# Hybrid encoder trunk on one core: passes of seven products that go on from chunk to chunk, and two pairs of the last chunk that join them

## The chip, the core and the metric

One core of one Trainium2 chip runs the whole program. The metric is the time of one execution on the device in microseconds (us), the median of three runs. Besides, one execution was recorded by the hardware profiler; its rows are what is called the trace here.

## What is computed

The reference is a trunk of two encoder layers on an input of 256 positions by 2048 channels, all in float32. Layer 0 mixes by multi-scale pooling and grouped-query attention, layer 1 by a bidirectional mLSTM. The mixers are not touched by the change. Each layer ends in a gated feed-forward block of width D_FF = 5632:

```python
def conv_ffn(x, w_up, conv_w, conv_b, w_down):
    u = x @ w_up
    up = jnp.pad(u, ((0, 0), (1, 1), (0, 0)))
    c = conv_w.astype(u.dtype)
    u = c[0] * up[:, :-2] + c[1] * up[:, 1:-1] + c[2] * up[:, 2:] + conv_b.astype(u.dtype)
    gate, val = jnp.split(u, 2, axis=-1)
    return (jax.nn.silu(gate) * val) @ w_down
```

`x = x + conv_ffn(rms_norm(x, norm_ffn[layer]), ...)` stands at the end of each layer. The change concerns the last product, the one with `w_down`, of 256 x 5632 by 5632 x 2048.

## The kernel before

**Numbers.** A float32 operand is held as two fp32r parts, a high part and a low rest. A product of two such operands is three matmuls: high by high, high by low, low by high.

**Weights.** All weights come in pieces of 128 x 1024 through one stream (class `Stream`, lines 86 to 151). `load` (line 95) issues a DMA on SP into one of six buffers, five pieces ahead of the piece in use. `split` (line 116) makes the two parts: a cast on ScalarE (line 127) and a subtraction on VectorE (line 128) into one of four `hl` buffers, two pieces ahead. The order of the pieces is fixed when the program is written, by `_ffn_weights` (line 1286).

**The feed-forward block.** `ffn_layer` (line 960) follows a plan that `_ffn_plan` (line 1232) writes out. The 5632 inner channels are 44 tiles in six chunks (`FCH`, line 33: 4, 8, 8, 8, 8, 8). An entry "up" makes one tile: 64 matmuls (`stat_group`), then on VectorE and ScalarE the sum of the parts (L427, L428), the norm's factor (L984), the convolution (L989 to L993), the gate (L997, L998) and the two parts of the result (L999, L1000). Every chunk's products with `w_down` are done one chunk later, between the up-tiles of the next chunk, so that weights and vector work are spread.

**Seven products for eight.** For a chunk in `BOTH` (line 35) both halves of the 2048 output columns, for the other chunks only half 1, are computed in the Strassen-Winograd manner: two tiles (a pair) by two blocks of 512 columns by two blocks of 128 positions, with seven products in place of eight. The entry "mix" (`combine`, line 1002) makes the sums of activations of one pair: four subtractions and additions on VectorE (L1006 to L1008) and their parts (L1012 on ScalarE, L1013 on VectorE). The sums of weights are made in two ways. For half 1 a DMA on SP loads one block and an accumulating DMA on POOL adds the other (class `Sum`, `prepare`, line 110, three buffers, up to ten pieces ahead); then VectorE adds that sum to the next piece twice (class `Chain`, L123 and L124). For half 0 they are premixed: `premix` (line 464) lets DMAs on the ScalarE queue and on POOL write them to memory ahead of time, paced by TensorE's progress, and the stream loads them like other weights.

**Passes A and B.** `unit` (line 1023) does the products of one or two pairs. A pass of kind A needs products 4, 6, 5, 3 and holds four PSUM banks, one of kind B needs 0, 1, 2 and holds three. The pool `ps` has four banks (line 226), so one pass is open at a time. A pass begins with the first pair of a chunk and ends with its last; then `drain` (line 1056) empties its banks on VectorE, one operation of 128 x 512 each (L1068; the first pass of a kind and half is copied on ScalarE instead, L1066, except where x takes it), into four running sums `acc` and into x. The next pass waits until the banks are free. For a chunk with both halves the order is A1 A1 B1 B1 A0 A0 B0 B0 (the digit is the half; each unit has two pairs and follows one up-tile; the up-tile with its unit is called a slot and has the up-tile's number). For a chunk with half 1 alone each unit has one pair, A four times and B four times, and after the second and fourth A unit one block of half 0 is done directly (`down`, line 1117).

**The end of the block.** The last chunk's four output blocks of 512 columns are done directly. `down_two` (line 1133) does blocks 0 and 1, first six tiles of each, then the last two, and `down` the blocks 2 and 3, 48 matmuls each; in layer 1 block 3 is done by `down_end` (line 1089), which stores each half as soon as it is ready. `total` (line 1078), eight additions on VectorE, brings the running sums of a half into x, after its last B pass; a block is added to x only behind the total of its half. In layer 0 each finished block of x is squared (L337), transposed on TensorE (L315) and split (L327, L330) for the next layer (`Norm`, line 304).

**Order.** TensorE's order is the program's. Drains, totals and norm steps are small tasks that a weave (line 154) puts between matmuls by a clock of its own. VectorE's, ScalarE's, SP's and POOL's orders are set by the framework's scheduler when the program is built; each engine then works in order.

Of the kernel before, what the change touches and what calls it, by code (L numbers as in the profile page):

```python
# [9 lines left out]
F32 = mybir.dt.float32  # L10
# [22 lines left out]
FCH = [4, 8, 8, 8, 8, 8]  # L33
CH = 8
BOTH = ((0, 2, 3, 4), (0, 1, 2, 3, 4))
NEG = -1.0e30
NGATE = 96 + 8
WARM = 5
# [47 lines left out]
class Stream:  # L86
# [123 lines left out]
def trunk(ctx: ExitStack, tc: tile.TileContext, gx, xT, xn, call, catt, cml, weights, mixes, out):  # L210
# [749 lines left out]
    def ffn_layer(layer, norm, nxt):  # L960
        with ExitStack() as es:
# [4 lines left out]
            st.sums = lp(f"ffs{layer}", 2)  # L966

            acc = kp.tile([P, 2, 4, 512], F32, tag="acc", name=f"acc{layer}")
            combos, pss, quads, seen = {}, {}, {}, set()

            conv = kp.tile([P, NC_CONV], F32, tag="conv", name=f"conv{layer}")
            a.dma_start(conv, call[:, NC_ALL + layer * NC_CONV : NC_ALL + (layer + 1) * NC_CONV])
# [47 lines left out]
                mm(ps, xl, wh, False, last)  # L1020
                wv.tick(0.68)

            def unit(kind, c, h, js):

                n = FCH[c] // 2
                order = (4, 6, 5, 3) if kind == "A" else (0, 1, 2)
                if js[0] == 0:
                    wv.until(lambda: "busy" not in pss)
                    for e in order:
                        pss[e] = psp.tile([P, 512], F32, tag="ps", name=f"pp{layer}_{c}_{h}{e}")  # L1030
                gt = gts[c]

                def part(j, k, t):
                    return [gt[:, 2 * j + k, i, t * P : t * P + P] for i in range(2)]


                todo = []
                for j in js:
                    s3, s1 = combos[c, j]
                    if kind == "A":  # L1040
                        xs = [[s3[:, i, m] for i in range(2)] for m in (1, 0, 2)] + [part(j, 1, 1)]
                    else:
                        xs = [part(j, 0, 0), part(j, 1, 0)]
                    todo += [(e, x_, j) for e, x_ in zip(order, xs)]
                if kind == "B":
                    todo += [(2, [combos[c, j][1][:, i] for i in range(2)], j) for j in js]
                for m, (e, x_, j) in enumerate(todo):
                    if m % 2 == 0:
                        hl = st.next()
                    wh, wl = (hl[:, i, m % 2 * 512 : m % 2 * 512 + 512] for i in range(2))  # L1050
                    product(pss[e], x_, wh, wl, j == 0, j == n - 1)
                if js[-1] == n - 1:
                    pss["busy"] = True
                    wv.add(drain(kind, c, h, order), 0.6)

            def drain(kind, c, h, order):

                x00, x01, x10, _ = parts_of_x(h)
                if kind == "A":
                    steps = [(acc[:, h, k], v.tensor_add, e) for k, e in enumerate(order[:3])]  # L1060
                    steps.append((x10, v.tensor_add, 3))
                else:
                    steps = [(acc[:, h, 3], v.tensor_add, 0), (x00, v.tensor_add, 1), (x01, v.tensor_sub, 2)]
                for to, op, e in steps:
                    if e in (4, 6, 5, 0) and (kind, h) not in seen:
                        a.copy(to, pss[e])  # L1066
                    else:
                        tc.keep_in_program_order(op(to, to, pss[e]))  # L1068
                    yield 1.6
                del pss["busy"]  # L1070
                seen.add((kind, h))
                if kind == "B" and c == len(FCH) - 2:
                    wv.add(total(h), 1.5)

            def parts_of_x(h):
# [40 lines left out]

            def down(c, b):
                gt, last = gts[c], c == len(FCH) - 1
                kts = list(range(FCH[c]))
                if last and nxt is None and b == NB - 1:  # L1120
                    down_end(gt, b, kts)
                    return
                ps = mmp.tile([P, 2, 512], F32, tag="mm", name=f"dn{layer}_{c}_{b}")
                mov_part(ps, lambda k: gt[:, k], kts, True, True)
                if last:
                    wv.until(lambda: ("total", 1) in pss)
                residual(ps, b)
                if last and nxt is None:
                    nc.sync.dma_start(out[:, :, b * 512 : b * 512 + 512], x[:, :, b * 512 : b * 512 + 512])
                elif last:  # L1130
                    nxt.add(b)

            def down_two(c):

                gt, n = gts[c], FCH[c]
                pss2 = [mmp.tile([P, 2, 512], F32, tag="mm", name=f"dn{layer}_{c}_{b}") for b in range(2)]
                for kts in (range(n - 2), range(n - 2, n)):
                    for ps in pss2:
                        mov_part(ps, lambda k: gt[:, k], list(kts), kts[0] == 0, kts[-1] == n - 1)
                wv.until(lambda: ("A", 0) not in seen or ("total", 0) in pss)  # L1140
                for b, ps in enumerate(pss2):
                    residual(ps, b)
                    if nxt is None:
                        nc.sync.dma_start(out[:, :, b * 512 : b * 512 + 512], x[:, :, b * 512 : b * 512 + 512])
                    else:
                        nxt.add(b)
# [3 lines left out]
            for kind, c, i, *j in _ffn_plan(layer):  # L1150
                if kind == "up":
                    if i == 0:
                        gts.append(actp.tile([P, 8, 2, S], F32R, tag=f"B{c % 2}", name=f"g{layer}_{c}"))
                    up(c, f, gts[c], i)
                    f += 1
                    if layer == 0 and c == len(FCH) - 1 and i == 4:
                        premix(1, 30.0, 30.0, 0)
                elif kind == "down":
                    down(c, i)
                elif kind == "two":  # L1160
                    down_two(c)
                elif kind == "mix":
                    combine(c, i)
                else:
                    unit(kind, c, i, *j)
# [19 lines left out]
def _mov(w):  # L1185

    return w.reshape(-1, 2, P, 512).transpose(0, 2, 1, 3).reshape(-1, P, CH * P)
# [38 lines left out]

def _halves(layer, c):

    return () if c in (-1, len(FCH) - 1) else (0, 1) if c in BOTH[layer] else (1,)


def _ffn_plan(layer):

    seq = []
    for c, n in enumerate(FCH):
        pairs = FCH[c - 1] // 2 if c else 0  # L1240
        halves = _halves(layer, c - 1)

        if halves == (0, 1):
            slots = [[(kind, c - 1, h, js)] for h in (1, 0) for kind in "AB"
                     for js in ((0, 1), (2, 3))[: pairs // 2]]
            slots = [[]] * (pairs < 4) + slots
        else:
            slots = [[(kind, c - 1, 1, (j,))] for kind in "AB" for j in range(pairs)]
            for b in range(2 if pairs else 0):
                slots[(b + 1) * pairs // 2 - 1].append(("down", c - 1, b))  # L1250

        busy = {j: k for k, slot in enumerate(slots) for u in slot if u[0] == "A" for j in u[3]}
        for i in range(n):
            seq.append(("up", c, i))
            seq += slots[i] if i < len(slots) else []
            if c < len(FCH) - 1:
                seq += [("mix", c, j) for j in range(n // 2) if i == max(2 * j + 1, busy.get(j, 0))]
    return seq + [("two", len(FCH) - 1, 0)] + [("down", len(FCH) - 1, b) for b in range(2, NB)]


def _down_chunks(layer, w):


    out, k0 = [], 0
    for c, n in enumerate(FCH):
        rows = w[k0 * P : (k0 + n) * P]
        blocks = [_mov(rows[:, b * 512 : b * 512 + 512]) for b in range(NB) if b // 2 not in _halves(layer, c)]
        if c == len(FCH) - 1:
            b0, b1 = blocks[:2]
            blocks[:2] = [b0[:-1], b1[:-1], b0[-1:], b1[-1:]]  # L1270
        out += blocks
        k0 += n
    n = sum(FCH[:-1]) // 2
# [12 lines left out]
def _ffn_weights(layer, up, parts):  # L1286
# [3 lines left out]
    for kind, c, i, *j in _ffn_plan(layer):  # L1290
# [1 line left out]
            out += up[u : u + 4]  # L1292
            u += 4
        elif kind in ("down", "two"):
            out += [next(down) for _ in range(FCH[c] // 2 * (2 if kind == "two" else 1))]
# [119 lines left out]
```

## Time and profile before

| | us |
|---|---|
| median of three runs | 2163.43 |
| lowest and highest | 2162.89, 2163.73 |
| the profiled execution | 2163.78 |
| span of its trace | 2162.0 |
| feed-forward block of layer 0 in the trace, about | 257 to 972 |
| feed-forward block of layer 1 in the trace, about | 1450 to 2162 |

In the profile PE is TensorE's matmuls, PEld its weight loads, DVE VectorE, ACT ScalarE, POOL GpSimd, SP the queue that issues most loads. L128 is line 128 of the kernel before. Tiles bear the program's names without numbers: `up` an up-tile's banks, `pp` those of a pass, `dn` and `end` those of direct blocks, `hl` a split piece of weights, `xt` a transposed piece of x, `xx` its parts. A row of the chain of waits says start, length and what worked; touching pieces of PE mean that TensorE waited for nothing.

### The profile page before, as it was taken

The numbers are of one execution on the slowest core, as the hardware profiler recorded it, in microseconds if no ns is written. First come the engines' busy times: TensorE is split into PE (matmuls) and PEld (weight loads), VectorE is DVE, ScalarE is ACT, GpSimd is POOL, SyncE is SP. The second block draws the span as 40 slices with busy tenths as digits, with TensorE's granted clock in tenths as the row PEclk, the third lists the DMA queues.
The fourth block names the chain that finished last, engine by engine and source line by source line (L and its number), as shares of the span: only waits on it lengthen the run. The fifth ranks groups of instructions, "written<-read, shape, count | busy, mean of one in ns | idle before, by whom it ended". The sixth has DMA issues, their size and how long they took to land.

```text
span 2162.0 us, 31902 instructions
## 1 busy us (share of the span) xinstructions
PE 2156.2 (100%) x11412; PEld 1844.2 (85%) x11412; DVE 1734.7 (80%) x2425; ACT 1414.3 (65%) x2208; POOL 212.7 (10%) x268
## 2 busy tenths in 40 slices
PE   9999999999999999999999999999999999999999
PEld 7888888888888888889888888888888888888887
DVE  7686688887988988986777676667889898988896
ACT  7665578766777767666454544457777777776763
POOL 0022111110100100001111111211100000000000
PEclk9999999999999999999999999999999999999999
DMA  9668989898999877779888888898978787887774
GB/s 323 213 202 250 287 250 311 248 280 247 298 296 293 287 257 232 266 232 252 231 246 251 237 250 230 273 276 249 289 226 285 258 283 246 265 262 251 233 249 162
DMA packets 164097, 555.29 MB, mean 257 GB/s; under 512 B 20602, under 2 KB 23202, under 8 KB 163938
## 3 DMA queue, kind: packets, MB, share of 16 engines
q1 hardware_dynamic: 129632, 462.88, 62.0%
q0 software_dynamic: 20704, 52.71, 14.8%
q10 hardware_dynamic: 13602, 37.67, 5.7%
q8 instruction: 89, 1.46, 0.3%
q14 instruction: 70, 0.57, 0.1%
HBM read 551.04 MB, written 69.25 MB: 287 GB/s over the span
## 4 chain that ended last, share of the span: by engine, by line
PE 97%; DVE 2%; DMA 1%; issue 0%; ACT 0%; DVEq 0%
PE up L264 44%; PE pp L264 15%; PE op L264 8%; PE dn L264 5%; PE mv L264 4%; PE mq L264 4%; PE mk L264 4%; PE mo L264 4%; PE qproj L264 3%; PE kproj L264 1%; PE vproj L264 1%; PE pool L264 1%; DVE hl L128 1%; PE qk L264 1%; PE av L264 1%; PE end L264 1%
## 5 line engine op out<-in xcount | busy, mean ns | idle before, releaser
L128 DVE TENSOR_TENSOR hl<-w,hl 128x1024 fp32r<-128x1024 f32 (+2 forms) x840 | 1009.4, 1214 | 218.4 <-ACT hl L127 216.0
L127 ACT CAST hl<-w 128x1024 fp32r<-128x1024 f32 (+2 forms) x839 | 863.4, 1047 | 451.4 <-PE up L264 145.3
L264 PE MATMUL up<-xx,hl 128*128 128x512 f32 (+1 forms) x5632 | 994.0, 337 | 0.0
L264 PEld LDWEIGHTS up<-xx,hl 128*128 128x128 f32 x5632 | 866.9, 188 | 130.9 <-DVE hl L128 0.5
L264 PE MATMUL pp<-hl,s 128*128 128x512 f32 x816 | 204.9, 392 | 0.3 <-DVE hl L128 0.3
L264 PEld LDWEIGHTS pp<-hl,s 128*128 128x128 f32 x816 | 150.4, 188 | 32.0 <-DVE hl L128 1.2
L473 POOL DMA_DIRECT2D m<-m x128 | 102.1, 800 | 701.0 <-PE up L264 293.1
L264 PE MATMUL pp<-hl,g 128*128 128x512 f32 x612 | 156.9, 391 | 0.0
L427 ACT COPY tb_up<-up 128x512 f32<-128x512 f32 x88 | 51.6, 587 | 123.4 <-PE up L264 123.2
L264 PEld LDWEIGHTS pp<-hl,g 128*128 128x128 f32 x612 | 112.2, 188 | 22.3
L991 ACT ACTIVATE y<-tb_up,conv 128x256 f32<-128x256 f32 x176 | 104.4, 593 | 0.0
L992 DVE TENSOR_TENSOR y<-y,z 128x510 f32<-128x510 f32 x88 | 60.7, 689 | 52.2 <-ACT y L991 52.2
L473 POOL DMA_DIRECT2D m<-in_dn x64 | 54.6, 853 | 468.1 <-PE dn L264 168.1
L264 PE MATMUL dn<-hl,g 128*128 128x512 f32 x432 | 100.3, 391 | 0.0
L428 DVE TENSOR_TENSOR tb_up<-up,tb_up 128x512 f32<-128x512 f32 x88 | 60.8, 691 | 49.2 <-ACT tb_up L427 48.9
L264 PEld LDWEIGHTS dn<-hl,g 128*128 128x128 f32 x432 | 80.6, 188 | 16.6
L989 ACT ACTIVATE z<-tb_up,conv 128x256 f32<-128x256 f32 x176 | 88.9, 505 | 5.1 <-DVE tb_up L984 4.2
L264 PE MATMUL mk<-xx,hl 128*128 128x512 f32 (+1 forms) x512 | 92.2, 337 | 0.0
L264 PE MATMUL mq<-xx,hl 128*128 128x512 f32 (+1 forms) x512 | 92.1, 337 | 0.0
L264 PE MATMUL mv<-hl,xx 128*128 128x512 f32 (+2 forms) x480 | 91.7, 350 | 0.0
L264 PE MATMUL op<-hl,cat 128*128 128x512 f32 x384 | 91.6, 393 | 0.0
L264 PE MATMUL mo<-hl,xx 128*128 128x512 f32 x384 | 90.5, 391 | 0.0
(232 smaller groups left out, 2196.5 us busy)
## 6 DMA issues: line engine op xcount, KB each, us to landing
w<-in_up SPq DMA_DIRECT2D x352, 512.0 KB, 4.8
w<-in_dn SPq DMA_DIRECT2D x176, 512.0 KB, 4.6
w<-in_m_in SPq DMA_DIRECT2D x124, 512.0 KB, 5.1
m<-in_dn ACTq DMA_DIRECT2D x128, 256.0 KB, 5.5
w<-m SPq DMA_DIRECT2D x64, 512.0 KB, 5.0
w<-in_a_in SPq DMA_DIRECT2D x46, 512.0 KB, 5.3
sum<-in_dn SPq DMA_DIRECT2D x36, 512.0 KB, 5.4
sum<-in_dn POOLq DMA_DIRECT2D x36, 512.0 KB, 9.1
```

The source lines that it names most:

```text
L127: (self.nc.vector.tensor_copy if i + c == 0 else self.nc.scalar.copy)(hl[:, 0, c : c + n], w[:, c : c + n])
L128: low = self.nc.vector.tensor_sub(hl[:, 1, c : c + n], w[:, c : c + n], hl[:, 0, c : c + n].bitcast(F32))
L264: last_mm[0] = pe.matmul(out_, lhsT, rhs, start=start, stop=stop, skip_group_check=True)
L427: a.copy(tb, ps[:, :, 1, :])
L428: v.tensor_add(tb, ps[:, :, 0, :], tb)
L473: paced(eng.dma_start(to[p : p + P // 2], src[p : p + P // 2], **kw))
L989: a.activation(z[:, 0, j, :], u[:, j, :], AF.Copy, scale=cw(tl, 0))
L991: a.activation(y[:, j, :], u[:, j, :], AF.Identity, scale=cw(tl, 1), bias=cw(tl, 3))
L992: v.tensor_add(y[:, :, 1:S], y[:, :, 1:S], z[:, 0, :, 0 : S - 1])
```

## The change

The order of the passes is written out per layer and chunk, a pass may go on over the chunk boundary, and the last chunk's first two pairs join the passes of half 1. Then its blocks 2 and 3 have only four tiles left to do directly.

```diff
+LAST = (4, 4)
+
+PASSES = (
+    ("B0 A0 B1 A1", "A1 B1", "B1 A1 A0 B0", "B0 A1 A0 B1", "A0 A1 A1+ B0 B1 B1+"),
+    ("B0 A1 A0 B1", "B1 A1 A0 B0", "B0 A1 A0 B1", "B1 A1 A0 B0", "A0 A1 A1+ B0 B1 B1+"),
+)
...
-            def unit(kind, c, h, js):
-
-                n = FCH[c] // 2
+            def unit(kind, c, h, js, first, last, end):
                 order = (4, 6, 5, 3) if kind == "A" else (0, 1, 2)
-                if js[0] == 0:
+                if first:
                     wv.until(lambda: "busy" not in pss)
...
-                    product(pss[e], x_, wh, wl, j == 0, j == n - 1)
-                if js[-1] == n - 1:
+                    product(pss[e], x_, wh, wl, first and j == js[0], last and j == js[-1])
+                if last:
                     pss["busy"] = True
-                    wv.add(drain(kind, c, h, order), 0.6)
+                    wv.add(drain(kind, h, order, end), 0.6)
...
-                if kind == "B" and c == len(FCH) - 2:
+                if end:
                     wv.add(total(h), 1.5)
...
-                kts = list(range(FCH[c]))
+                kts = list(range(_direct(layer, c, b), FCH[c]))
...
-            def down_two(c):
+            def down_two(c, second):
                 gt, n = gts[c], FCH[c]
-                pss2 = [mmp.tile([P, 2, 512], F32, tag="mm", name=f"dn{layer}_{c}_{b}") for b in range(2)]
-                for kts in (range(n - 2), range(n - 2, n)):
-                    for ps in pss2:
-                        mov_part(ps, lambda k: gt[:, k], list(kts), kts[0] == 0, kts[-1] == n - 1)
+                if not second:
+                    twos.extend(mmp.tile([P, 2, 512], F32, tag="mm", name=f"dn{layer}_{c}_{b}") for b in range(2))
+                parts = [(ps, kts) for kts in (range(n - 2), range(n - 2, n)) for ps in twos]
+                for ps, kts in parts[1:] if second else parts[:1]:
+                    mov_part(ps, lambda k: gt[:, k], list(kts), kts[0] == 0, kts[-1] == n - 1)
+                if not second:
+                    return
...
+def _pairs(layer, c):
+
+    return (LAST[layer] if c == len(FCH) - 1 else FCH[c]) // 2
+
+
+def _direct(layer, c, b):
+
+    return LAST[layer] if c == len(FCH) - 1 and b >= NB // 2 else 0
...
 def _ffn_plan(layer):
...
+    slots, late, units = [[] for _ in range(FT)], [], []
+    at = 1
+    for c in range(len(FCH) - 1):
+        at = max(at + (c == 0) * FCH[0], sum(FCH[: c + 1]))
+        step = len(_halves(layer, c))
+        for pas in PASSES[layer][c].split():
+            k = c + pas.endswith("+")
+            for j in range(0, _pairs(layer, k), step):
+                units.append((pas[0], k, int(pas[1]), tuple(range(j, j + step))))
+                to = slots[min(at, FT - 1)] if at <= FT else late
+                to.append(len(units) - 1)
+                if step == 1 and pas[0] == "A" and j % 2:
+                    to.append(("down", c, j // 2))
+                at += 1
+    for n, u in enumerate(units):
+        first, last = (not 0 <= m < len(units) or (units[m][0], units[m][2]) != (u[0], u[2]) for m in (n - 1, n + 1))
+        units[n] = u[:4] + (first, last, all(o[2] != u[2] for o in units[n + 1 :]))
...
+    seq += [("two", c, 0)] + [units[e] for e in late] + [("two", c, 1)]
+    return seq + [("down", c, b) for b in range(2, NB)]
```

A sign "+" in `PASSES` marks a unit of the next (the last) chunk. Two passes of the same kind and half that follow each other become one. In layer 0 these are A1 from chunk 0 to 1, B1 from chunk 1 to 2 and B0 from chunk 2 to 3; in layer 1 B1 from 0 to 1, B0 from 1 to 2 and B1 from 2 to 3. With the last chunk the slots 36 to 43 hold A0, A0, A1, A1, A1 (the last chunk's two pairs), B0, B0, and in slot 43 two B1 units. The last chunk's B1 unit stands between the first and the second part of `down_two`. The listing of the pieces (`_down_chunks`, `_ffn_weights`) follows the new plan; each engine's order of work is again made by the scheduler.

Counted over the program, TensorE has 84 matmuls more on `pp` and 72 and 24 fewer on `dn` and `end`. VectorE has 19 operations fewer in drains and 34 more in splits, chain additions and combinations. ScalarE has 14 more, SP six loads more, and POOL four accumulating DMAs more.

More of the change, by code (lines that the diff above doesn't have):

```diff
@@ L968, in ffn_layer @@
             acc = kp.tile([P, 2, 4, 512], F32, tag="acc", name=f"acc{layer}")
-            combos, pss, quads, seen = {}, {}, {}, set()
+            combos, pss, quads, seen, twos = {}, {}, {}, set(), []
             conv = kp.tile([P, NC_CONV], F32, tag="conv", name=f"conv{layer}")
@@ L1050, in unit, with drain @@
                     wh, wl = (hl[:, i, m % 2 * 512 : m % 2 * 512 + 512] for i in range(2))
-                    product(pss[e], x_, wh, wl, j == 0, j == n - 1)
-                if js[-1] == n - 1:
+                    product(pss[e], x_, wh, wl, first and j == js[0], last and j == js[-1])
+                if last:
                     pss["busy"] = True
-                    wv.add(drain(kind, c, h, order), 0.6)
-            def drain(kind, c, h, order):
+                    wv.add(drain(kind, h, order, end), 0.6)
+            def drain(kind, h, order, end):
                 x00, x01, x10, _ = parts_of_x(h)
@@ L1131, in down @@
                     nxt.add(b)
-            def down_two(c):
+            def down_two(c, second):
                 gt, n = gts[c], FCH[c]
-                pss2 = [mmp.tile([P, 2, 512], F32, tag="mm", name=f"dn{layer}_{c}_{b}") for b in range(2)]
-                for kts in (range(n - 2), range(n - 2, n)):
-                    for ps in pss2:
-                        mov_part(ps, lambda k: gt[:, k], list(kts), kts[0] == 0, kts[-1] == n - 1)
+                if not second:
[5 more added lines that the diff above has]
+                    return
                 wv.until(lambda: ("A", 0) not in seen or ("total", 0) in pss)
-                for b, ps in enumerate(pss2):
+                for b, ps in enumerate(twos):
                     residual(ps, b)
@@ L1160, in ffn_layer @@
                 elif kind == "two":
-                    down_two(c)
+                    down_two(c, i)
                 elif kind == "mix":
@@ L1227, in _halves @@
 def _halves(layer, c):
-    return () if c in (-1, len(FCH) - 1) else (0, 1) if c in BOTH[layer] else (1,)
-def _ffn_plan(layer):
-    seq = []
-    for c, n in enumerate(FCH):
[L1240 to L1252, printed above, removed]
+    return () if c == len(FCH) - 1 else (0, 1) if c in BOTH[layer] else (1,)
@@ new lines, in _pairs @@
+def _pairs(layer, c):
+    return (LAST[layer] if c == len(FCH) - 1 else FCH[c]) // 2
+def _direct(layer, c, b):
+    return LAST[layer] if c == len(FCH) - 1 and b >= NB // 2 else 0
+def _ffn_plan(layer):
+    slots, late, units = [[] for _ in range(FT)], [], []
[15 more added lines that the diff above has]
+        units[n] = u[:4] + (first, last, all(o[2] != u[2] for o in units[n + 1 :]))
+    slots = [[e if isinstance(e, tuple) else units[e] for e in slot] for slot in slots]
+    busy = {(u[1], j): f for f, slot in enumerate(slots) for u in slot if u[0] == "A" for j in u[3]}
+    seq, f0 = [], 0
+    for c, n in enumerate(FCH):
@@ L1253, in _ffn_plan @@
         for i in range(n):
             seq.append(("up", c, i))
[L1255 to L1258, printed above, removed]
+            mixes = [(busy.get((c - 1, j), 0) - f0, ("mix", c, j)) for j in range(_pairs(layer, c))]
+            mixes = [(k, e) for k, e in mixes if i == max(2 * e[2] + 1, k)]
@@ L1261, in _down_chunks @@
+            soon = [e for k, e in mixes if c == len(FCH) - 1 and k < i]
+            seq += soon + slots[f0 + i] + [e for _, e in mixes if e not in soon]
+        f0 += n
+    seq += [("two", c, 0)] + [units[e] for e in late] + [("two", c, 1)]
+    return seq + [("down", c, b) for b in range(2, NB)]
 def _down_chunks(layer, w):
@@ L1266, in _down_chunks @@
         rows = w[k0 * P : (k0 + n) * P]
-        blocks = [_mov(rows[:, b * 512 : b * 512 + 512]) for b in range(NB) if b // 2 not in _halves(layer, c)]
+        blocks = [_mov(rows[_direct(layer, c, b) * P :, b * 512 : b * 512 + 512]) for b in range(NB) if b // 2 not in _halves(layer, c)]
         if c == len(FCH) - 1:
@@ L1272, in _down_chunks @@
         k0 += n
-    n = sum(FCH[:-1]) // 2
+    n = (sum(FCH[:-1]) + LAST[layer]) // 2
     res = [np.concatenate(out)]
@@ L1294, in _ffn_weights @@
         elif kind in ("down", "two"):
-            out += [next(down) for _ in range(FCH[c] // 2 * (2 if kind == "two" else 1))]
+            n = FCH[c] // 2 - 1
+            out += [next(down) for _ in range((n, n + 2)[i] if kind == "two" else (FCH[c] - _direct(layer, c, i)) // 2)]
         elif kind != "mix":
```

## Prediction

> **What bounds the kernel now.** I read the page first, then who waited for whom, then the chain of work that ended last.
>
> ```profile
> span 2162.0 us, 31902 instructions
> ...
> PE 2156.2 (100%) x11412; PEld 1844.2 (85%) x11412; DVE 1734.7 (80%) x2425; ACT 1414.3 (65%) x2208; POOL 212.7 (10%) x268
> ...
> PE 97%; DVE 2%; DMA 1%; issue 0%; ACT 0%; DVEq 0%
> ```
> ```profile
> PEld pp L264 <- DVE hl L128: 1.2, 2, 0.7
> ```
> ```profile
> 528.42 11.15 PE up L264 x64
> ...
> 555.94 8.55 DMA w<-in_dn
> ...
> 575.52 11.14 PE up L264 x64
> ...
> 697.62 4.37 PE pp L264 x19
> ...
> 703.43 11.27 PE up L264 x64
> ...
> 797.95 11.14 PE up L264 x64
> ...
> 1695.83 5.53 PE pp L264 x24
> 1701.36 11.14 PE up L264 x64
> 1712.50 4.10 PE pp L264 x18
> ```
> ```profile
> 2114.72 32.64 PE dn L264 x144
> 2147.36 10.89 PE end L264 x48
> ```
>
> TensorE is the path. A slot of the plan is one up-tile (64 matmuls, 11.14 us) and one unit: an A unit of two pairs costs 24 matmuls in 5.53 us, a B unit 18 in 4.10, a direct matmul 10.89 / 48 = 0.227. In layer 1 these pieces touch each other to the end. Waiting shows in two places of layer 0 only. From 528.42 + 11.15 = 539.57 the plan holds 9 B matmuls, two up-tiles and two A units, 2.05 + 22.28 + 11.06 = 35.39 us, and the next up-tile starts after 35.95: 0.56 lost, behind a 512 KB load that took 8.55. From 697.62 to 703.43 the A unit takes 5.81 instead of 5.53, and the up-tile behind it 0.13 more: 0.4. So about 1.0 us of waiting is all that could be removed in the two FFN layers.
>
> **The change part by part.**
>
> *Fewer matmuls.* Of each layer's last chunk, 48 direct matmuls go (24 in each of the blocks 2 and 3: 48 x 0.227 = 10.89 us), and one A unit and one B unit come (5.53 + 4.10 = 9.63). That is -1.26 per layer, **-2.5 us** for two. The listed program of the changed kernel counts the same: pp +84 matmuls, dn -72, end -24, so 12 fewer.
>
> [...]
>
> *Fewer drains.* Three passes per layer continue the pass before them (A1, B1, B0 in layer 0; B1, B0, B1 in layer 1), and 19 VectorE additions of 128x512 go. TensorE never waits for a drain in the trace, so I price this at 0. The cover is the 11.14 us up-tile ahead of each unit. It cannot bring more than the 1.0 us above.
>
> *More work for VectorE, and moved.* Four pairs more: 6 more splits, 8 more chain additions (L123, L124), 20 more operations of the combinations; in all 15 operations more than before. Where they fall matters more than their number.
>
> ```profile
> 1997.66 1.22 DVE L128 TENSOR_TENSOR hl<-sum,hl 128x1024 fp32r<-128x1024 f32 x1
> 1998.80 0.42 DVE L1006 TENSOR_TENSOR sf<-s 128x256 f32<-128x256 f32 x1
> 1999.13 0.68 DVE L428 TENSOR_TENSOR tb_up<-up,tb_up 128x512 f32<-128x512 f32 x1
> 1999.73 0.41 DVE L1000 TENSOR_TENSOR g<-s,g 128x256 fp32r<-128x256 f32 x1
> 2000.14 1.23 DVE L128 TENSOR_TENSOR hl<-w,hl 128x1024 fp32r<-128x1024 f32 x1
> 2001.29 0.28 DVE L1007 TENSOR_TENSOR sf<-sf,s 128x128 f32<-128x128 f32 x1
> 2001.49 0.68 DVE L984 TENSOR_TENSOR tb_up<-tb_up,R 128x512 f32<-128x512 f32 x1
> 2002.09 2.35 DVE L128 TENSOR_TENSOR hl<-w,hl 128x1024 fp32r<-128x1024 f32 x2
> ```
> ```profile
> 2000.84 2.22 PE L264 MATMUL pp<-hl,s 128*128 128x512 f32 x9
> 2002.90 0.86 PE L264 MATMUL pp<-hl,g 128*128 128x512 f32 x3
> 2003.60 0.62 PE L264 MATMUL up<-xx,hl 128*128 128x512 f32 x2
> ```
> ```profile
> 1987.10:2003.76 16.66, 16.66 (x89) 14.23 (x89) 16.62 (x24) 11.48 (x16) 0.85 (x1) 1.00 0.73 211
> ```
>
> Back to back, starts are 1.14 us apart for a split, 0.60 for 128x512, 0.34 for 128x256, 0.20 for 128x128 (0.47 for 128x384 is an estimate between these). By starts an up-tile takes VectorE 4 x 1.14 + 4 x 0.60 + 2 x 0.34 = 7.64, an A unit of half 1 (which sums its weights here) 4 x 1.14 + 4 x 0.60 = 6.96, of half 0 4.56, a B unit 3.42, a pair's combination 0.34 + 2 x 0.20 + 0.47 + 0.20 = 1.41, an A drain 2.4, a B drain 1.8. What a slot leaves over (16.67 us with A, 15.24 with B):
>
> - before, the worst: A1 behind a B drain, 16.67 - 7.64 - 6.96 - 1.8 = +0.27 (the window above, VectorE 16.62 of 16.66); A0 behind a B drain with two combinations -0.15.
> - after, in the middle chunks: A1 behind a B drain again, +0.27; A0 now stands behind A1, so its drain is 2.4: -0.75. In the listed order of the new program the combination has slipped behind later splits there, and each split of the next up-tile has from 1.3 us less to 0.6 us more ahead of it than before. Price 0.
> - after, in the last chunk: A0 A0 A1 A1 A1 in a row. Slot 38 (A1, A drain, one combination) -1.74, slot 39 (A1, one combination) +0.66, slot 40 +2.07.
>
> How late may VectorE be? In the window above the fourth split of the A unit ends at 2001.37 and its matmuls begin about 2000.84 + 6 x 0.23 = 2002.2, so 0.8 us ahead; the next up-tile's first split, due at 2003.60, ends near 2003.3, 0.3 ahead. Slot 38 has 2.0 us more to do. In the listed order 0.8 of it stands ahead of the A unit's fourth split, and 0 ahead of the next up-tile's first. I take 0.3 us of waiting per layer, **+0.6**, between 0 and 2.0 - 0.3 = 1.7 per layer. The two B units that share slot 43 find VectorE a few us ahead after the light B slots 41 and 42 (15.24 - 7.64 - 3.42 = +4.2 each before drains), price 0, at most 1.
>
> *Sums and DMAs.* Four more sums: each a load on SP and an accumulating DMA on POOL, and two plain loads more on SP.
>
> ```profile
> sum<-in_dn SPq DMA_DIRECT2D x36, 512.0 KB, 5.4
> ...
> sum<-in_dn POOLq DMA_DIRECT2D x36, 512.0 KB, 9.1
> ```
> ```profile
> 787.87 0.78 POOL L473 DMA_DIRECT2D m<-m  x1 [15.85 <-PE up L264]
> ```
>
> Behind a sum that waits for one of its three buffers stand the up-tile's loads on SP. The fourth sum of consecutive A1 units is due 16.67 + 2.77 us after the first was used and needs 5.4 + 9.1 = 14.5: it fits, as before with two units in a row; the third adds nothing new. In layer 0 the last chunk's A0 moves from slot 40 to slot 36 (up-tile at 797.95), and reads sums that POOL's premixing writes; their last step was issued at 787.87, and its data is due in slot 37, past 812. Price 0. The waits of layer 0 (1.0 us) belong to the time in which premixing runs beside the A1 units; these units move by two slots within that time. I leave 1.0 standing, between 0 and 4.
>
> *The end of layer 0.* Blocks 2 and 3 shrink from 48 to 24 matmuls, and block 2 needs the whole total of half 1, whose last B unit now stands between the two parts of the last chunk's direct blocks. In the new order TensorE does block 2, the 16 transposes of blocks 0 and 1, 18 matmuls of block 3, then transposes block 2 of x.
>
> ```profile
> 955.52 1.65 DVE L330 SCALAR_TENSOR_TENSOR xx<-xt,gcol,xx 128x256 fp32r<-128x256 f32 x4
> ...
> 971.98 1.28 DVE L437 TENSOR_TENSOR x<-x,dn 128x512 f32<-128x512 f32 x2 [0.17 <-PE dn L264]
> 973.18 1.05 DVE L128 TENSOR_TENSOR hl<-w,hl 128x864 fp32r<-128x864 f32 x1
> ```
> ```profile
> 957.90 0.83 ACT L327 ACTIVATE xx<-xt,gcol 128x256 fp32r<-128x256 f32 x2
> ...
> 962.43 0.64 ACT L337 ACTIVATE sq<-x 128x512 f32<-128x512 f32 x1
> 962.97 0.19 ACT L337 ACTIVATION_READ_ACCUMULATOR sq<-x 128x1 f32 x1
> ```
> ```profile
> 964.21 0.44 PE xt L315 x4
> ```
>
> Counted from block 2's last matmul, TensorE comes back for that transpose after 4 x 0.44 + 18 x 0.227 = 5.85 us. VectorE must by then have done 0.17 + 0.60 (one half of the residual), a split (about 1.0), eight low parts of 0.41, two steps of the total and the other half of the residual (1.8): 6.9, and it waits for ScalarE, which makes each low part's high part (0.42) and one square (0.8) between: about 0.8 more, 7.7. **+1.8 us**, between 0 and twice as much. In layer 1 nothing is transposed, and the last additions and stores follow the last matmul as before.
>
> *Sum:* -2.5 + 0.6 + 1.8 = -0.1. The profiled execution took 2163.78 (2162.0 of span), 0.35 more than the median of 2163.43; taken from the median, **2163.3 us**.
>
> **The rivals.**
>
> *All cover holds.* ScalarE and VectorE interleave better at the end of layer 0, and slots 38 to 40 pass: -2.5, 2160.9. For it: in layer 1 a slot with +0.27 left no gap.
>
> *VectorE becomes the bound.* If operations follow each other only at full duration, 0.08 us is added to each. Slot 38 (27 operations) then lacks 1.74 + 2.2 = 3.9, slot 39 1.2, slot 40 gains 0.6: 5.1 in arrears, of which 1.4 is free (the A1 slot of before lacks as much by this count, without a gap): 3.7 us per layer. The A0 slots behind A1, five in all, would lack 0.75 + 1.9 on top of 0.8 left from the A1 slots, 3.5, of which the 2.0 that before's A0 slot lacks are free: 1.5 each. Together 14.9 in place of 0.6: 2177.6. It decides from the point where a slot's arrears exceed VectorE's lead, about 2 us. Against it: starts stand 0.08 closer than durations wherever nothing is waited for.
> [...]
>
> *Transfers in layer 0.* Two A1 units and two A0 units in a row while premixing runs, and the 8.55 us load comes more often: +3 for the loads, 2166.3.
>
> *The hand-over costs.* Each of the six merged passes spares TensorE a wait for free PSUM banks that the trace hides: it could be at most the 1.0 us of waiting, 2162.3. That the passes don't merge is excluded: the 19 drain additions are gone from the program.
>
> **How the numbers follow.** Forecast 0.52, all cover holds 0.25, transfers 0.12, VectorE bound 0.08, hand-over 0.03. The likeliest is 2163.3. The bounds of the terms are -2.5 - 1.0 below and, above, 3.6 + 3.4 + 1 + 3 - 2.5 = +8.5, all at once; the range that leaves 2 in 10 out goes from 2160.3 to 2168.0. A measurement of this kernel tells about 0.2%, 4.3 us, from no change. Faster by that needs more than all removed matmuls and all waits together (3.5): 0.03. Slower by that needs 2167.8: the VectorE rival and a bad draw of the transfers, 0.11. Within: 0.86.
>
> **What would show it.** Right: layer 1's pieces dense, with slots 38 to 40 within a us of 3 x 16.67; a gap of 1 to 3 us ahead of the transposes of block 2 at the end of layer 0, released by DVE x; the tail behind the last matmul unchanged. Wrong: waits of TensorE for hl of more than 1 us in many slots (VectorE), waits in layer 0's A1 units behind DMA (transfers), or a layer 1 that is shorter by more than 1.3 us.

## The result and the profile after

The changed kernel takes **2174.68 us** (median of 5 runs, 2172.97 to 2175.63) against 2163.43 for the kernel before (5 runs, 2162.89 to 2163.92): a ratio of 1.0050, 95% interval 1.0039 to 1.0061. It is 11 us slower, where no change was forecast. The profiled execution took 2175.2 us.

The page of the changed kernel (span; busy time of each engine; share of the chain that ended last by engine):

```profile
span 2173.3 us, 31942 instructions
...
PE 2159.0 (99%) x11400; PEld 1843.5 (85%) x11400; DVE 1739.5 (80%) x2440; ACT 1421.4 (65%) x2222; POOL 214.9 (10%) x272
...
PE 90%; DVE 5%; DMA 3%; issue 1%; ACT 1%; DVEq 0%; POOLq 0%; ACTq 0%
```

12 matmuls have gone, yet the span grew by 11.3. The chain that ended last, 97% TensorE before, now runs through VectorE for 5% and through DMAs for 3%. Busy sums hardly move: VectorE has 4.8 us more work in 2173. So the loss isn't a busier engine on average; it has to be looked for as waits. Who waited for whom (engine, line, released by: us in total, times, longest), for TensorE's matmuls and its weight loads:

```profile
PE pp L270 <- DVE s L1019: 5.3, 2, 2.9
PE up L270 <- DVE hl L134: 1.5, 3, 0.9
...
PE xt L321 <- DVE x L443: 1.1, 1, 1.1
```
```profile
PEld pp L270 <- DVE s L1019: 6.2, 2, 3.3
```

Two waits, one in each layer, hold about half of the loss, and none of this kind stood in the profile before: a pass waits not for its weights (`hl`) but for `s`, the combination of activations. TensorE's timeline (start, length, what, and in brackets the idle time ahead and its releaser) has them in slot 40, in the unit of the joined pairs:

```profile
876.46 2.24 PE L270 MATMUL pp<-hl,s 128*128 128x512 f32 x9
...
879.60 0.72 PE L270 MATMUL pp<-hl,s 128*128 128x512 f32 x2 [0.21 <-ACT s L1018]
...
883.20 2.82 PE L270 MATMUL pp<-hl,s 128*128 128x512 f32 x7 [2.88 <-DVE s L1019]
...
887.10 6.29 PE L270 MATMUL up<-xx,hl 128*128 128x512 f32 x34
...
2073.58 2.24 PE L270 MATMUL pp<-hl,s 128*128 128x512 f32 x9
...
2079.91 1.89 PE L270 MATMUL pp<-hl,s 128*128 128x512 f32 x7 [2.45 <-DVE s L1019]
...
2082.33 3.87 PE L270 MATMUL up<-xx,hl 128*128 128x512 f32 x21
```

The first pair's 12 matmuls run densely (those on `g` are left out here); at the third matmul of the second pair (tiles 38 and 39), the first that takes a low part, TensorE stands. The unit lasts 887.10 - 876.46 = 10.64 us in layer 0 and 2082.33 - 2073.58 = 8.75 in layer 1, where 5.53 was priced: +5.1 and +3.2, together **8.3 us**. Layer 0 pays more because its wait is 0.4 us longer and, above all, because its matmuls are slow for a while after it (the last section).

VectorE's timeline of layer 0 shows why the low part is late:

```profile
869.16 2.35 DVE L134 TENSOR_TENSOR hl<-w,hl 128x1024 fp32r<-128x1024 f32 x2
873.09 0.69 DVE L129 TENSOR_TENSOR w<-w,sum 128x512 f32<-128x512 f32 x1 [1.57 <-DMA sum<-in_dn]
...
874.84 0.42 DVE L1004 TENSOR_TENSOR s<-s,y 128x256 f32<-128x256 f32 x1
...
879.52 0.28 DVE L1014 TENSOR_TENSOR sf<-sf,s 128x128 f32<-128x128 f32 x1
879.72 1.22 DVE L134 TENSOR_TENSOR hl<-w,hl 128x1024 fp32r<-128x1024 f32 x1
880.85 0.69 DVE L990 TENSOR_TENSOR tb_up<-tb_up,R 128x512 f32<-128x512 f32 x1
881.46 1.22 DVE L134 TENSOR_TENSOR hl<-w,hl 128x1024 fp32r<-128x1024 f32 x1
882.59 0.76 DVE L1019 TENSOR_TENSOR s<-sf,s 128x384 fp32r<-128x384 f32 x2
```

Two things are to be seen. VectorE stands 1.57 us for a sum (0.93 in layer 1), and all that is queued behind it moves back, the gate of tile 39 (L1004) too. And between the last `sf` (879.52) and the low parts (L1019, 882.59) its in-order queue holds two splits and a step of up-tile 40, 3 us of work that TensorE needs later: the first split is the unit's own last piece, due five matmuls (1.1 us) after the low part, the second belongs to up-tile 41. The rest of the 11.3 + 2.5 = 13.8 us lies in smaller gaps: 1.2 at the transpose of block 2, 1.6 in slot 8 of layer 1, some 0.5 more than before up to slot 37 of layer 0 (its new waits stand in slots 24 and 25), 0.4 in slot 38 of each layer, 0.5 in up-tile 40 of layer 1, and 0.2 to 0.5 in slot 43.

### The profile page after: what moved, and what is told of

It reads as the page before. It is cut to its first block, busy times and chain, and to the rows that moved or that the text cites. A ratio compares the mean times of both kernels' runs of the same rounds, so it can differ in the third digit from the quotient of the medians.

```text
span 2173.3 us, 31942 instructions
## 1 busy us (share of the span) xinstructions
PE 2159.0 (99%) x11400; PEld 1843.5 (85%) x11400; DVE 1739.5 (80%) x2440; ACT 1421.4 (65%) x2222; POOL 214.9 (10%) x272
## 4 chain that ended last, share of the span: by engine, by line
PE 90%; DVE 5%; DMA 3%; issue 1%; ACT 1%; DVEq 0%; POOLq 0%; ACTq 0%
PE up L270 40%; PE pp L270 13%; PE op L270 8%; PE mv L270 4%; PE mq L270 4%; PE mk L270 4%; PE mo L270 4%; PE dn L270 4%; PE qproj L270 3%; DVE hl L134 2%; DMA sum<-in_dn 1%; DMA w<-in_up 1%; PE kproj L270 1%; PE vproj L270 1%; DMA w<-in_dn 1%
## 5 line engine op out<-in xcount | busy, mean ns | idle before, releaser
L134 DVE TENSOR_TENSOR hl<-w,hl 128x1024 fp32r<-128x1024 f32 (+1 forms) x842 | 1011.5, 1214 | 228.3 <-ACT hl L133 221.7
L270 PE MATMUL pp<-hl,s 128*128 128x512 f32 x864 | 219.9, 395 | 6.1 <-DVE s L1019 5.3
L270 PEld LDWEIGHTS pp<-hl,s 128*128 128x128 f32 x864 | 158.9, 188 | 43.0 <-DVE s L1019 6.2
L270 PE MATMUL pp<-hl,g 128*128 128x512 f32 x648 | 166.7, 392 | 0.0
L270 PEld LDWEIGHTS pp<-hl,g 128*128 128x128 f32 x648 | 119.6, 188 | 24.0
L119 POOL DMA_DIRECT2D sum<-in_dn x40 | 34.9, 876 | 571.2 <-DMA sum<-in_dn 255.9
L270 PE MATMUL op<-hl,mcat 128*128 128x512 f32 x384 | 89.5, 392 | 0.0
```

The lines of the kernel that those rows point to most:

```text
L119: self.nc.gpsimd.dma_start(w, self.srcs[i].other, accum_op=ALU.add)
L134: low = self.nc.vector.tensor_sub(hl[:, 1, c : c + n], w[:, c : c + n], hl[:, 0, c : c + n].bitcast(F32))
L270: last_mm[0] = pe.matmul(out_, lhsT, rhs, start=start, stop=stop, skip_group_check=True)
```

## The experiments

Theory 1: the joined unit takes the combination of tiles 38 and 39 one slot after up-tile 39, and in VectorE's queue it can't be ready by then. Theory 2: three A1 units in a row need one sum more than three buffers supply, and VectorE's wait for it is the cause. Theory 3: the merged order of passes costs most. Theory 4, which arose from the first results: VectorE's whole load in the last chunk. Every edit also lets the scheduler order VectorE's work anew, so a run can differ in more than the place that is named. "Slots" and line numbers are the changed kernel's.

### Which half of the change: merge_only, join_only

```diff
 # merge_only
-LAST = (4, 4)
+LAST = (0, 0)
-    (..., "A0 A1 A1+ B0 B1 B1+"),
+    (..., "A0 A1 B0 B1"),
 # join_only
-    ("B0 A0 B1 A1", "A1 B1", "B1 A1 A0 B0", "B0 A1 A0 B1", "A0 A1 A1+ B0 B1 B1+"),
+    ("A1 B1 A0 B0", "A1 B1", "A1 B1 A0 B0", "A1 B1 A0 B0", "A0 A1 A1+ B0 B1 B1+"),
 # and layer 1 in the same way
```

> No pair of the last chunk joins (its weights go through the plain down products as before the change); the passes of the chunks before it go on from chunk to chunk as in the changed kernel. Theory 1 (joining costs, merging does not): 2163 to 2166 us, of it at most 2.5 us in slots 24 and 25 of layer 0 and in up-tile 8 of layer 1, which the trace of the changed kernel shows as new waits. Theory 3 (the merged order, with A0 units right behind A1 units, costs the larger part): 2168 us or more.

> The chunks before the last one keep the order of passes of the kernel before, with no pass that goes on; the last chunk joins as in the changed kernel. Theory 1 and theory 2 (all of the loss is in the last chunk): 2171 to 2174 us, with the waits at slot 40 of both layers. Theory 3 (the merged order costs the larger part): 2163 to 2166 us.

merge_only: 2165.62 us, ratio 1.0007 (0.9998 to 1.0015). join_only: 2172.72 us, ratio 1.0039 (1.0026 to 1.0052). Theory 3 falls: the larger part belongs to the last chunk. Merging alone can't be told from no change by the time; its trace has a few waits in up-tiles that the kernel before doesn't have there (1.3 us in all), and those of join_only stand in slot 40 as in the changed kernel. TensorE's waits, first merge_only, then join_only:

```profile
PE up L270 <- DVE hl L134: 1.3, 2, 0.8
```
```profile
PE pp L270 <- DVE s L1019: 4.6, 2, 2.9
PE pp L270 <- ACT s L1018: 1.5, 2, 1.0
```

### The due time or the sums: late_pair, light_sums

```diff
 # late_pair, both layers
-"A0 A1 A1+ B0 B1 B1+"
+"A0 B0 A1 A1+ B1 B1+"
 # light_sums: in prepare, for the joined unit's sums
-        self.nc.gpsimd.dma_start(w, self.srcs[i].other, accum_op=ALU.add)
+        if self.srcs[i].both:
+            self.nc.gpsimd.dma_start(w, self.srcs[i].other, accum_op=ALU.add)
```

> Both layers' last passes stand as A0 B0 A1 A1+ B1 B1+: the joined A unit moves from slot 40 to slot 42, nothing else changes. Theory 1 (the joined unit takes the combination of the last chunk's second pair, tiles 38 and 39, one slot after up-tile 39, so TensorE waits for it): both waits at that unit go, 3.3 us and the slow matmuls behind them in layer 0 and 2.9 us in layer 1, about 8 us together; 2166 to 2168 us. Theory 2 (three A1 units in a row ask for one sum more than the three buffers can make ahead, and VectorE stands in its queue for it): the three still stand in a row, so a wait of 2 to 3 us per layer comes back at slot 42; 2172 to 2176 us.

> The changed kernel, but the joined A unit's sums are only loaded, not added to: the second load of the pair that GpSimd issues is left out, for two sums in each layer, so the output lacks these addends. The sum of the joined unit is then in its buffer some 8 us sooner. Theory 1 (the combination is due one slot after its tile, whatever VectorE waited for earlier): the waits at slot 40 stay at 2 us or more per layer; 2171 to 2175 us. Theory 2 (VectorE's 1.57 and 0.93 us in its queue for that sum push the combination back): the waits at slot 40 shrink by at least that, to under 1.7 us, and with them the slow matmuls of layer 0; 2167 to 2170 us.

light_sums: 2172.14 us, ratio 1.0035 (1.0022 to 1.0047). TensorE's waits between 870 and 892 us, then between 2065 and 2100 (lines are one higher in this kernel):

```profile
PE pp L271 <- DVE s L1020: 1.4, 1, 1.4
PE pp L271 <- ACT s L1019: 0.2, 1, 0.2
```

Both layers gave these same two rows. The waits for the low part went from 2.88 and 2.45 to 1.4 and 1.4: the late sum makes 1.5 and 1.0 us of them, about what VectorE had stood, and theory 2 is right by that much. The rest stays with no sum late, and VectorE's timeline shows it in theory 1's place:

```profile
877.06 0.28 DVE L1015 TENSOR_TENSOR sf<-sf,s 128x128 f32<-128x128 f32 x1
877.40 1.23 DVE L135 TENSOR_TENSOR hl<-w,hl 128x1024 fp32r<-128x1024 f32 x1
878.54 0.69 DVE L991 TENSOR_TENSOR tb_up<-tb_up,R 128x512 f32<-128x512 f32 x1
879.14 1.22 DVE L135 TENSOR_TENSOR hl<-w,hl 128x1024 fp32r<-128x1024 f32 x1
880.28 0.75 DVE L1020 TENSOR_TENSOR s<-sf,s 128x384 fp32r<-128x384 f32 x2
```

From the last `sf` to the low parts stand the same two splits and the same step. Neither theory's whole claim held: theory 1's time did, its "2 us or more" did not; theory 2's "under 1.7" did, its time did not.

late_pair: 2169.64 us, ratio 1.0026 (1.0015 to 1.0038), some 5 us less than the changed kernel and 2 more than theory 1 wanted. No wait for `s` is left. At slot 42 VectorE doesn't stand for a sum either, though three A1 units are still in a row, so theory 2's wait didn't come back. With two slots more the combination is in time, and that although VectorE has more to do there (below): the due time is what made the waits. But others came, nearly all for splits:

```profile
PE pp L270 <- DVE hl L134: 3.6, 6, 1.0
PE xt L321 <- DVE x L443: 1.6, 1, 1.6
...
PE dn L270 <- DVE hl L134: 0.7, 1, 0.7
```

### Out of VectorE's queue: pool_combine, pool_late

```diff
 # combine; pool_late has late_pair's order as well
+w_ = nc.gpsimd if c == len(FCH) - 1 else v
-v.tensor_sub(sf[:, 0:2], g4[:, 0::3], ...)
+w_.tensor_sub(sf[:, 0:2], g4[:, 0::3], ...)
 # so too the other two steps of sf and the low parts
```

> The changed kernel, with the five subtractions and additions of each combination of the last chunk (two pairs per layer) on GpSimd; ScalarE's two copies in it stay. Theory 1 (the combination stands in VectorE's in-order queue behind splits and the next up-tile's first step, and TensorE needs it one slot after its tile): out of that queue it is ready about 2 us after the silu of tile 39 plus GpSimd's own time, so the waits at slot 40 shrink from 3.3 and 2.9 us to below 1.5 us each: 2167 to 2171 us, the lower end if the slow matmuls behind layer 0's wait go as well. Theory 4 (what counts is the sum of VectorE's work in the last chunk, some 2.8 us of it now gone in each layer, not the queue's order): about the same saving but the splits of slots 38 to 40 come earlier too. Rival (GpSimd's operations take longer than the queue did, or hold up the second loads of the sums that it issues): no gain, 2174 us or more.

> Both edits: the joined A unit at slot 42, and the last chunk's combinations on GpSimd. With the joined unit at slot 42 alone, waits for splits remained: 0.9 us in slot 41 of both layers, 0.8 us at the first down product behind layer 0's last unit and 1.2 us at slot 43 of layer 1. If these come from VectorE's load in the last chunk (theory 4), 2.8 us less of it in each layer takes them to 0.4 us or less: 2165 to 2168 us. If they come from waits for ScalarE or for sums inside VectorE's queue, they stay: 2169 to 2170 us.

pool_combine: 2172.04 us, ratio 1.0038 (1.0025 to 1.0050). In slot 40 the waits for `s` are gone, and 0.5 and 0.9 us of waits for splits stand there instead: theory 1's mechanism. In layer 0 VectorE's wait for the sum is gone as well, but in layer 1 it still stood 1.51 us for it, so that isn't what removed the waits. The time is outside its range, because 1.5 us of new waits came in slot 38 of layer 0, and as much in layer 1: ScalarE's in-order queue, in which copies of the combination stand ahead of casts of weights, now waits for GpSimd, two of whose operations took 2.25 and 3.44 us there. TensorE's waits between 840 and 850 us:

```profile
PE pp L270 <- DVE hl L134: 0.8, 1, 0.8
PE pp L270 <- ACT hl L133: 0.7, 1, 0.7
```

pool_late: 2182.94 us, ratio 1.0087 (1.0074 to 1.0101), a miss for both theories. GpSimd's timeline:

```profile
875.78 11.44 POOL L1020 TENSOR_TENSOR s<-sf,s 128x384 fp32r<-128x384 f32 x1 [0.91 <-ACT s L1019]
...
887.97 0.86 POOL L119 DMA_DIRECT2D sum<-in_dn  x1
...
889.94 1.41 POOL L1020 TENSOR_TENSOR s<-sf,s 128x384 fp32r<-128x384 f32 x2
```

One low part took 11.44 us (9.82 in layer 1), and a sum's second load, which GpSimd issues, stood behind it; TensorE then waited 4.0 us at once in each layer for ScalarE's cast of that sum. So the price of the rival named for pool_combine, "no gain", was too mild, and the run says nothing on theory 4.

### What late_pair still loses: late_light, late_lean

late_light is late_pair with light_sums' edit. late_lean is late_pair with this:

```diff
 # total
+                    if h:
+                        tc.keep_in_program_order(op(to, to, e))
-                    tc.keep_in_program_order(op(to, to, e))
```

> The joined A unit at slot 42, and its two sums per layer only loaded, without the second addend that GpSimd's load adds (the output lacks it). If VectorE still waits for late sums there (theory 2), the four remaining waits of 0.8 to 1.2 us go: 2165 to 2167 us. If its load alone is the bound (theory 4), nothing changes: 2169 to 2170 us.

> The joined A unit at slot 42, and the eight steps that combine the first half's products (0.60 us each on VectorE, 4.8 us per layer, which the trace of the run with the joined unit at slot 42 shows between slots 40 and 42) left out, so columns 0 to 1023 lack them. Theory 4 (with the unit at slot 42 VectorE's load is the bound): the wait of 0.9 us in slot 41 of both layers goes, and the 0.8 us at the first down product and 1.2 us at slot 43 shrink or go: 2166 to 2168 us. Rival (single waits in VectorE's queue, not its load): nothing changes, 2169 to 2170 us.

late_light: 2169.73 us, ratio 1.0029 (1.0019 to 1.0040), the same as late_pair; its gaps in slots 41 and 43 are those of late_pair within 0.02 us. With the unit at slot 42 no late sum matters there. late_lean: 2168.24 us, ratio 1.0021 (1.0012 to 1.0029), between the two ranges and not to be told from late_pair by the time. What tells is the busy time in two windows (window and length, then us and instructions of PE, PEld, DVE, ACT, POOL; granted clock, DMA share, GB/s), for late_pair, then late_lean:

```profile
866.00:892.00 26.00, 25.79 (x138) 21.52 (x137) 26.00 (x38) 15.74 (x23) 1.72 (x2) 1.00 0.85 248
2059.00:2085.00 26.00, 25.79 (x138) 21.53 (x138) 26.00 (x38) 15.71 (x23) 1.71 (x2) 1.00 0.85 257
```
```profile
866.00:892.00 26.00, 26.00 (x140) 22.25 (x139) 25.48 (x35) 17.40 (x26) 1.72 (x2) 1.00 0.87 283
2059.00:2085.00 26.00, 26.00 (x137) 22.12 (x136) 24.31 (x34) 18.69 (x29) 1.74 (x3) 1.00 0.83 264
```

In late_pair VectorE is busy for 26.00 of 26.00 us in both layers: with the total of half 0, which this order brings beside the A1 units, it has become the bound, and TensorE waits. Without that total VectorE has air, and the wait of slot 41 goes in both layers: theory 4 holds there. It doesn't hold for everything: the 0.8 us behind layer 0's last unit and the 1.6 at the transpose stay, slot 43 of layer 1 shrinks only from 1.2 to 0.8, and in layer 1 a transfer of a sum that took 9.76 us brought new waits of 2.5 us, which eat the rest of the gain.

### One pair instead of two: one_pair, one_pair_old

```diff
-LAST = (4, 4)
+LAST = (2, 2)
-                units.append((pas[0], k, int(pas[1]), tuple(range(j, j + step))))
+                units.append((pas[0], k, int(pas[1]), tuple(range(j, min(j + step, _pairs(layer, k))))))
 # the pieces are packed for an odd number of pairs as well
 # one_pair_old: PASSES as in join_only
```

> Only the first pair of the last chunk (tiles 36 and 37) joins, in both layers; tiles 38 and 39 go through the plain down products. The matmuls saved are half, 6 of 12. Theory 1 (the second pair is due one slot after its last tile): no wait for a combination at slot 40, since tile 37 ends three slots ahead; with half the added VectorE work and one sum less, 2166 to 2168 us, of which 1.2 us is the half saving that is missing. Theory 2 (the fifth sum in a row is what comes late): the wait for it stays and pushes back the splits of slots 39 and 40 by 1 us or more in each layer, 2168 to 2171 us.

> Only tiles 36 and 37 join, and the chunks before keep the order of passes of the kernel before, with no pass that goes on. If the run with the merged order and one joined pair lost its 3 us by the merged order (waits of 1.3 us in layer 0 and 2.2 us in layer 1, at places where the kernel before has at most 0.5 us), this gives 2163 to 2165 us, the same as before. If the joining of one pair loses it, 2166 to 2168 us.

one_pair: 2166.96 us, ratio 1.0013 (1.0004 to 1.0022). TensorE is dense in slot 40, here in layer 0:

```profile
876.24 2.24 PE L270 MATMUL pp<-hl,s 128*128 128x512 f32 x9
878.32 0.85 PE L270 MATMUL pp<-hl,g 128*128 128x512 f32 x3
879.01 11.30 PE L270 MATMUL up<-xx,hl 128*128 128x512 f32 x64
```

Theory 1's forecast. A pair whose tiles ended three slots ago costs nothing there; the pair from tiles 38 and 39, with all that it brings, is what made the difference of 7.7 us. For theory 2 the run is no test: the late sum of the changed kernel is the sixth of its row (the second of the joined unit), and here only five are made. one_pair_old: 2164.64 us, ratio 1.0003 (0.9994 to 1.0012), span 2162.0, as before. By the traces, what one_pair still loses belongs to the merged order (2.2 us in slots 7 and 8 of layer 1, 1.2 in slot 24 of layer 0; one_pair_old has no such waits), though the intervals of the two runs overlap. In one_pair_old the 6 matmuls that are saved (1.3 us, estimated from 0.227 each) go into small waits at the end of layer 0 and in slots 38 and 43. No version found beats the kernel before; the most that joining could bring is 2.5 us, 0.12%, below what a measurement tells here.

## Why the prediction was wrong

- *Fewer matmuls* (-2.5): right, 11412 became 11400, and an up-tile without a wait still takes 11.14 us.
- *Fewer drains* (0): no gain, as forecast. The merged order itself is not free in the trace (slot 8 of layer 1; slots 24 and 25 of layer 0): some 2 us here, 1 in merge_only, 2.5 in one_pair, for which the prediction had only the A0 slots' "price 0". Which instruction makes those waits was not settled: in the changed kernel the chain at up-tile 8 goes through a load of 12.58 us, in merge_only through ScalarE and VectorE alone.
- *More work for VectorE, and moved* (+0.6): **this step failed**, at its last line, "slot 40 +2.07". The ledger set a slot's work against a slot's length, and the due times that followed it were those of splits alone. A combination was counted as load, not as an input; the second one was even booked in slot 39, while the trace has all of it in slot 40 (from 876.91 in layer 0). In the kernel before, and in half of the joined unit, a pair is complete two or more slots ahead of its A unit; the last pair is complete one slot ahead, and a positive balance of 2 us doesn't bring its low parts to the front of an in-order queue. The unit cost 5.1 and 3.2 us more in place of 0, of which 1.5 and 1.0 belong to the late sum of the next point and about 1.6 in layer 0 to the slow clock. light_sums shows that the rest comes without a late sum, late_pair that two more slots remove it, one_pair that it goes with the last pair. No run put the low parts ahead of the two splits and changed nothing else, so what the queue's order alone is worth stays open. For slots 38 and 39, 0.3 us per layer was forecast; from up-tile to up-tile, 0.4 in layer 0 and 0.5 in layer 1 are seen.
- *Sums and DMAs* (0): "it fits ... the third adds nothing new" failed too, for the sixth sum of the three units, by 1.57 and 0.93 us. The chain of layer 0:

```profile
858.12 6.08 DMA sum<-in_dn
...
864.75 8.32 DMA sum<-in_dn
...
873.09 0.69 DVE w L129
```

  The 14.5 us that a sum needs was well sized (873.09 - 858.12 = 14.97). The due time was not: VectorE wanted it at 873.09 - 1.57 = 871.52, 13.4 us after the buffer came free, and not 19.4: the prediction counted from the moment when the sum that had the buffer before "was used"; VectorE first used it at 850.36, but its last use, a split, ended only at 858.1. Layer 0's transfers (0 to +4) stayed small, about +0.5.
- *The end of layer 0* (+1.8): right in place and releaser, 1.2 in size.
- *The rivals.* "VectorE becomes the bound" (2177.6) is nearest in time but not what happened: what follows a split still starts 1.13 us after it (881.46 and 882.59 above), the A0 slots cost little, and over the 26 us from 866 and from 2059 us VectorE is busy for 23.52 and 25.03 us, against 24.61 and 24.38 in the kernel before; only within the wait itself it has no pause. That rival is near to what late_pair turned into, though there by the total of half 0 and not by slower operations. Missing was the one that came: an input that is due too soon.

## What to carry to other kernels

When a unit of work is moved towards the end of a pipeline, list every operand that it takes with the moment it is complete and the moment it is due, not only the load of each engine per slot; an operation on the path can wait behind work with more time in a queue that is in order, as the low parts did in slot 40 behind two splits and a step of up-tile 40, 3 us of work. A prefetch that "needs 14.5 us" has to be set against the time between the last use of the old data and the first use of the new by the engine that works ahead, not by the engine that is the bound. Taking work to another engine to empty a queue can move the wait to whatever that engine also issues, as in pool_late, where TensorE waited 4.0 us at once in each layer.

## What the runs showed of the hardware

**The clock after a wait.** The granted clock (behind the five busy times) in the changed kernel:

```profile
883.20:887.10 3.90, 3.90 (x10) 3.04 (x11) 3.77 (x6) 2.11 (x4) 0.00 (x0) 0.59 0.80 243
...
2079.80:2083.70 3.90, 3.79 (x18) 3.19 (x19) 3.87 (x7) 3.32 (x6) 0.00 (x0) 1.00 0.84 242
```

After layer 0's wait TensorE does 10 matmuls in 3.90 us, at 0.59 of its clock; after layer 1's, 18 in the same time. That is about 1.6 us (0.41 of 3.90) on top of the wait. In light_sums two waits of the same 1.4 us differ, layer 1 slow, layer 0 not:

```profile
2074.20:2078.30 4.10, 4.07 (x11) 3.25 (x12) 3.79 (x6) 3.05 (x7) 0.00 (x0) 0.60 0.76 228
...
880.90:884.80 3.90, 3.90 (x19) 3.29 (x20) 3.53 (x5) 3.77 (x7) 0.00 (x0) 1.00 0.75 237
```

So the length of one wait doesn't decide it. In the changed kernel the slow stretch of layer 0 is 3.41 us long, at 0.50. The rows are that stretch, the 3.41 us ahead of it, and for layer 1 the 3.41 us ahead of the first matmul behind the wait and the 3.41 us from that matmul's start:

```profile
883.87:887.28 3.41, 3.41 (x10) 2.64 (x9) 3.28 (x5) 1.44 (x2) 0.00 (x0) 0.50 0.83 245
880.46:883.87 3.41, 0.67 (x3) 0.58 (x4) 3.41 (x6) 2.92 (x7) 0.00 (x0) 1.00 0.50 154
2076.50:2079.91 3.41, 0.75 (x3) 0.30 (x2) 3.41 (x6) 2.94 (x7) 0.00 (x0) 1.00 0.33 109
2079.91:2083.32 3.41, 3.41 (x16) 2.86 (x17) 3.38 (x5) 2.83 (x6) 0.00 (x0) 1.00 0.84 227
```

In light_sums, layer 1, the slow stretch and the 3.41 us ahead of it give:

```profile
2071.63:2075.04 3.41, 1.75 (x7) 0.97 (x7) 3.41 (x6) 3.41 (x8) 0.00 (x0) 1.00 0.47 167
2075.04:2078.45 3.41, 3.41 (x10) 2.63 (x9) 3.10 (x5) 2.36 (x5) 0.00 (x0) 0.50 0.80 240
```

How long TensorE was busy in the 3.41 us ahead doesn't decide it either: 1.75 us in layer 1 of light_sums, and the clock falls to 0.50; 0.75 us in layer 1 of the changed kernel, and it stays at 1.00. What makes it fall these runs don't show.

**GpSimd beside a busy VectorE.** The same low part took 11.44 us in pool_late, while VectorE was busy for 10.54 of 11.40 us, and at 889.94 one of this size and a smaller one took 1.41 us together. The busy times of that window:

```profile
875.80:887.20 11.40, 11.19 (x60) 9.16 (x59) 10.54 (x14) 2.94 (x3) 11.40 (x1) 1.00 0.92 290
```

What VectorE did there were splits and additions of two inputs, one behind the other until 886.34, and the low part was done at 887.22. Whether VectorE's operations held it up was not shown. It isn't always GpSimd's operation that takes longer: in pool_combine, beside a low part on GpSimd from 848.82 to 850.65, a step of 128x512 on VectorE (L990, from 849.68) took 1.51 us, and the same step of the changed kernel (from 848.41) 0.69.
